# Local attention's output product: from sixteen full products to seven half-size block products per column group, with the work behind it moved into the scheduler

## The chip, the cores and the metric

The kernel runs on one core of one Trainium2 chip. The metric is the device time of one execution in microseconds (us), the median of three runs; lower is better. Five engines of the core work side by side, each through its own list of instructions in a fixed order: TensorE (PE in the rows) multiplies matrices, VectorE (DVE) and GpSimd (POOL) do elementwise work, ScalarE (ACT) does activations and copies, and SyncE (SP) issues most of the transfers (DMA). An instruction waits at the head of its engine's list until what it needs is there, and what stands behind it waits with it.

## The reference

The reference is one decoder block over 1024 positions of width 1024 in float32. Local attention (A, eight heads of 64 in a window of 128) and latent attention (B, eight heads) both read projections of the normed input; each has an output product, a gate, and the gated sum goes through one more product before a feed-forward part:

```
o_a = swa_sink_attention(qa, ka, va, swa_sinks[l])
o_b = mla_attention(q_nope, q_rope, k_nope, k_rope, vb)
y = jax.nn.sigmoid(g_a) * (o_a @ w_o_swa[l]) + jax.nn.sigmoid(g_b) * (o_b @ w_o_mla[l])
x = x + y @ w_out[l]
h = rmsnorm(x, ffn_norm_g[l])
x = x + (jax.nn.silu(h @ w_gate[l]) * (h @ w_up[l])) @ w_down[l]
```

`o_a` and `o_b` are 1024 x 512, `w_o_swa` and `w_o_mla` 512 x 1024, `w_out` 1024 x 1024.

## The kernel before

Every float32 operand of a product is split into a high and a low part in the engine's own number format: ACT casts the high part, DVE or POOL subtracts it from the source for the low part (`split`, and `lower` inside the scheduler). A product of two such operands is three matmuls per 128 rows of the contraction (`mm3`): high by high, high by low, low by high. A matmul has 128 x 128 weights and 512 columns. So "12 matmuls" below are one block of 128 x 512 outputs with a contraction of 512, and "6 matmuls" one with a contraction of 256.

The program goes through these stages, in us of the profiled execution:

- up to 318: projections, and the heads of local attention between products for the gates (`fa`, `fb`);
- 318 to 352: the plan `pre`: transposes of the latents (`lT`), rope products (`r`), the last gate products (`fb` with weights `wl`). The gate products are copied out of PSUM by ACT (`go`) and stored to `gate_d`;
- 352 to 531: latent attention, 8 heads by 8 query blocks, issued by `plan`. A block is a score product (`scb`), the row maximum (DVE), exp (ACT, `p`), a scale (POOL), transposes (`pTb`) whose results are split (`pth` by ACT, `ptl` by DVE), and the product with the values (`ob`). Between them stand the last products of queries and keys, and the output product of local attention, called oA: eight of its sixteen outputs (`mix_steps`, `G`), each 12 matmuls, copied out by ACT to `ar`;
- 531 to 599.8: the loop `steps`, written out by hand: the other eight oA (`mix_a`) and the sixteen outputs oB of latent attention (`mix_b`). There `gate` rows are loaded (`sg`), put through a sigmoid by ACT, multiplied by oA (four whole rows by POOL, L1847, eight halves by DVE, L1500) and by oB (DVE, L1852), added (DVE, L1853), split into `yh` and `yl`, and summed into the block sums of y (DVE, `y_sums`). `W_WORK` builds the block sums of `w_out` (tiles `wo`) beside it: loads, negations by ACT, and accumulating transfers (`w_acc`, from POOL's queue: the destination is added to in flight);
- from 599.8: the product with `w_out`, called xo, as seven block products over sums of blocks of y and w_out, and then the feed-forward part.

`Plan` is a list scheduler in the program that writes the kernel: every step has an engine, a cost in ns, the steps it follows, a rank and pool slots that it takes and gives back; the order in which the steps are picked is the order of the instructions on each engine. A load of weights is a step of SP with a cost of 400 ns (`w0`). The time at which the chip really does a step plays no part in it. `U` and `V` are two pools of SBUF slots.

## Time and profile before

| what | value |
|---|---|
| median of 3 runs | 1321.35 us (1320.81 to 1322.18) |
| the profiled execution | 1320.95 us, of which the span from the first to the last instruction is 1319.2 us and 1.75 us lie around it |
| PE, busy | 1306.1 us, 99% of the span |
| DVE, ACT, POOL, busy | 70%, 49%, 43% |
| mean granted clock of TensorE | 0.997 of full speed |

The profile comes from one execution. A busy share says how much of the span an engine worked; with PE at 99% the time is above all the number of matmuls times the pitch from one to the next, and what can be had beside that are PE's few gaps.

### The profile page before, as it was taken

The page shows a single profiled execution, that of the slowest core. Times are in us where ns is not written, and L with a number is a line of the kernel's source. Part 1 is how long each engine was busy: PE and PEld are TensorE (multiplying, and loading weights), DVE is VectorE, ACT ScalarE, POOL GpSimd, SP SyncE. Part 2 cuts the span into 40 slices and gives each one's busy share as a digit, 9 for nine tenths or more (in the row PEclk, how much of TensorE's full clock was granted, in tenths as well). Part 3 has the DMA queues.
Part 4 walks back from the last instruction along what each step waited for, and adds up shares of the span by engine and source line. Part 5 has one row for each costly group of instructions (what it writes and reads, how often), then busy time and mean ns, then how long its engine had stood idle before and what let it go on. Part 6 is the DMA issues. An engine that isn't in the chain of part 4 may idle for free.

```text
span 1319.2 us, 18715 instructions
## 1 busy us (share of the span) xinstructions
PE 1306.1 (99%) x6463; PEld 1102.4 (84%) x6463; DVE 919.9 (70%) x1514; ACT 643.2 (49%) x1301; POOL 566.4 (43%) x552
## 2 busy tenths in 40 slices
PE   9999999999999999999999999999999999999997
PEld 6899888887888888888888888888888888888886
DVE  7869777765778885589889755766566555663962
ACT  7434666665477787545464322232223323644452
POOL 2116666553333267310134467775566621022520
PEclk9999999999999999999999999999999999999999
DMA  9454332436410022896231336743454335996503
GB/s 375 161 187 154 117 111 85 132 105 211 143 30 17 25 81 81 309 265 191 84 124 49 126 139 222 260 178 133 180 183 162 134 119 201 386 361 225 178 24 134
DMA packets 81246, 210.49 MB, mean 160 GB/s; under 512 B 9408, under 2 KB 16064, under 8 KB 80448
## 3 DMA queue, kind: packets, MB, share of 16 engines
q1 hardware_dynamic: 78416, 202.48, 43.4%
q0 software_dynamic: 1440, 4.72, 1.9%
q10 hardware_dynamic: 1296, 2.10, 0.5%
q8 instruction: 51, 0.84, 0.3%
q14 instruction: 43, 0.35, 0.1%
HBM read 143.34 MB, written 61.73 MB: 155 GB/s over the span
## 4 chain that ended last, share of the span: by engine, by line
PE 96%; DVE 1%; issue 1%; ACT 1%; DMA 1%; POOLq 0%; POOL 0%; SPq 0%; ACTq 0%; DVEq 0%
PE fa L269 8%; PE fa L267 8%; PE fa L268 8%; PE fb L267 6%; PE fb L269 6%; PE fb L268 6%; PE fd L268 5%; PE fd L267 5%; PE fd L269 5%; PE pTb L1580 2%; PE xo L268 2%; PE xo L267 2%; PE xo L269 2%; PE ob L1618 1%; PE scb L1535 1%; PE ob L1617 1%
## 5 line engine op out<-in xcount | busy, mean ns | idle before, releaser
L261 DVE TENSOR_TENSOR wl<-wr,wl 128x512 fp32r<-128x512 f32 x147 | 143.4, 997 | 67.6 <-ACT wl L260 67.2
L261 DVE TENSOR_TENSOR lrv<-lr,lrv 128x1024 fp32r<-128x1024 f32 x77 | 105.1, 1396 | 49.6 <-ACT lrv L260 48.2
L260 ACT CAST lrv<-lr 128x1024 fp32r<-128x1024 f32 x77 | 80.2, 1052 | 95.2 <-PE fd L269 70.7
L267 PE MATMUL fd<-lrv 128*128 128x512 f32 x308 | 119.8, 389 | 0.0
L268 PE MATMUL fd<-lrv 128*128 128x512 f32 x308 | 119.8, 389 | 0.0
L269 PE MATMUL fd<-lrv 128*128 128x512 f32 x308 | 119.8, 389 | 0.0
L260 ACT CAST wl<-wr 128x512 fp32r<-128x512 f32 x147 | 85.2, 620 | 3.6 <-DVE wr L962 1.7
L1564 POOL TENSOR_SCALAR p<-p,denb 128x384 f32<-128x384 f32 (+3 forms) x64 | 47.9, 750 | 86.8 <-DVE denb L1560 72.2
L261 DVE TENSOR_TENSOR wl<-sm,wl 128x512 fp32r<-128x512 f32 x59 | 52.1, 907 | 35.1 <-ACT wl L260 35.0
L275 POOL TENSOR_TENSOR wr<-wr,sm 128x512 f32<-128x512 f32 x20 | 30.5, 1529 | 97.5 <-DVE wl L261 97.5
L267 PEld LDWEIGHTS fd<-lrv 128*128 128x128 f32 x308 | 57.8, 188 | 12.1
L269 PEld LDWEIGHTS fd<-lrv 128*128 128x128 f32 x308 | 57.8, 188 | 12.0
L268 PEld LDWEIGHTS fd<-lrv 128*128 128x128 f32 x308 | 57.8, 188 | 11.9
L397 POOL TENSOR_SCALAR ms<-ss 128x1 f32<-128x1 f32 x32 | 10.4, 324 | 112.8 <-ACT xn L2131 62.8
L2043 ACT ACTIVATE act<-sm 128x512 f32<-128x512 f32 x11 | 7.0, 633 | 104.1 <-DVE sm L272 104.1
L272 DVE TENSOR_TENSOR ptl<-pTb,pth 128x512 fp32r<-128x512 f32 (+2 forms) x96 | 49.5, 548 | 8.7 <-ACT pth L1591 8.4
L275 POOL TENSOR_TENSOR sm<-wr,wr 128x512 f32<-128x512 f32 (+1 forms) x36 | 41.6, 1162 | 30.6 <-PE fb L269 26.1
L1555 ACT ACTIVATE p<-scb,nmb 128x384 f32<-128x384 f32 (+3 forms) x64 | 47.8, 748 | 13.0 <-DVE nmb L1550 9.0
L1550 DVE CUSTOM_DVE_ANT_0 scb<-scb,mask 128x384 f32<-128x384 f32 (+3 forms) x64 | 48.3, 760 | 6.9 <-PE scb L1537 6.3
L267 PE MATMUL fb<-t3h,wl 128*128 128x512 f32 x120 | 48.1, 401 | 0.0
L1591 ACT CAST pth<-pTb 128x512 fp32r<-128x512 f32 (+2 forms) x96 | 43.1, 484 | 9.9 <-PE pTb L1580 9.4
L268 PE MATMUL fb<-t3l,wl 128*128 128x512 f32 x120 | 47.4, 395 | 0.0
(403 smaller groups left out, 4258.1 us busy)
## 6 DMA issues: line engine op xcount, KB each, us to landing
lr<-la_d SPq DMA_DIRECT2D x77, 256.0 KB, 5.4
wr<-in_w_gate_dram SPq DMA_DIRECT2D x22, 512.0 KB, 4.4
wr<-in_w_up_dram SPq DMA_DIRECT2D x22, 512.0 KB, 5.1
la_d<-sd SPq DMA_DIRECT2D x22, 512.0 KB, 5.1
wd<-in_w_down_dram SPq DMA_DIRECT2D x22, 512.0 KB, 6.5
rb_d<-wd SPq DMA_DIRECT2D x22, 512.0 KB, 2.6
lr<-rb_d SPq DMA_DIRECT2D x44, 256.0 KB, 5.4
lr<-in_w_down_dram SPq DMA_DIRECT2D x33, 256.0 KB, 5.4
```

The lines of the kernel that those rows point to most:

```text
L260: nc.scalar.copy(hi, src)
L261: (eng or nc.vector).tensor_tensor(lo, src, hi.bitcast(F32), op=ALU.subtract)
L267: nc.tensor.matmul(ps, ah, bh, start=first and i == 0, stop=False, skip_group_check=go_on)
L268: nc.tensor.matmul(ps, ah, bl, start=False, stop=False, skip_group_check=go_on)
L269: nc.tensor.matmul(ps, al, bh, start=False, stop=last and i == n - 1, skip_group_check=go_on)
L272: eng.tensor_tensor(out, a, b, op=ALU.subtract)
L275: eng.tensor_tensor(out, a, b, op=ALU.add)
L1550: nc.vector.tensor_tensor_reduce(s_, s_, m_, 1.0, -NEG, op0=ALU.add, op1=ALU.min, accum_out=nm)
L1555: nc.scalar.activation(p_, s_, AF.Exp, scale=-1.0, bias=t_.pop(("nm", key)), accum_out=den)
L1564: nc.gpsimd.tensor_scalar(p[:, 0:w], p[:, 0:w], den, 0.0, op0=ALU.mult, op1=ALU.add)
L1580: nc.tensor.transpose(pp[:, k], t_["p", key][:, blk(4 * g + k)], ident)
L1591: nc.scalar.copy(hi, pp)
```

## The change

The product oA is computed as seven block products per group of 128 output columns, in place of four full-size blocks of sums: the contraction of 512 and the 1024 positions are both cut in two, and sums of blocks of `o_a` (seven operand sets) are multiplied by sums of blocks of `w_o_swa`. There are four pairs of column blocks (j), so 28 products of 6 matmuls. The operand sets are made during the first heads of latent attention (`set_steps`): `oa` is loaded, POOL makes eight block differences (`os`), ACT and POOL split the seven sets (`oh`, `ol`), SP stores them to DRAM (`set_d`, 14 stores) and fetches them before use (`oas`, seven loads of 1 MB). Per j, POOL makes the sums of the weights (`wsum`, four operations), and these are split too. The seven products are added up on their way out of PSUM (`block_out`): two copies by ACT and five adds by DVE.

Everything of the hand-written loop becomes steps of `plan` (`post_steps`): loads of gates and sigmoids, all eight multiplications of a gate row by oA on POOL, the oB products, the sums, the splits of y, the block sums of y (half as additions on POOL, half as accumulating transfers from POOL's queue) and the sums of `w_out` with their splits, whose low parts go to POOL. The engine "Q" in the plan stands for the accumulating transfers. The plan now counts slots of U and V; slack and ranks are other numbers; the first xo product takes its low parts of y last.

```diff
-    TAIL = {"E": 0, "D": 80, "A": 100, "P": 36, "S": 0}
-    HOP = {"E": 70, "D": 36, "A": 36, "P": 79, "S": 50}
+    TAIL = {"E": 0, "D": 80, "A": 100, "P": 36, "S": 0, "Q": 8500}
+    HOP = {"E": 70, "D": 36, "A": 36, "P": 79, "S": 50, "Q": 0}
...
+                        if sum(x < busy for x in slots[pool]) < n + self.more[name][2]:
+                            t = busy
...
-    for nm, dp in (("oa", 0), ("oa", 1), ("oa", 2), ("ob", 0), ("ob", 1), ("oa", 3), ("ob", 2), ("ob", 3)):
+    for nm, dp in (("oa", 0), ("oa", 1), ("oa", 2), ("oa", 3), ("ob", 0), ("ob", 1), ("ob", 2), ("ob", 3)):
...
-    pre = Plan(30)
+    pre = Plan(0)
...
-    plan = Plan(30)
+    plan = Plan(45)
-    LOW = {'Q': 'P', 'u': 'P', 'o': 'P', 'b': 'P', 'w': 'P'}
+    LOW = {'Q': 'P', 'u': 'P', 'o': 'P', 'b': 'P', 'w': 'P', 'n': 'D', 'os': 'P', 'ws': 'P', 'Ba': 'D', 'ya': 'P', 'y': 'D', 's': 'P'}
...
+    R_HALF = {1: (0, 0), 2: (2, 0), 4: (2, 1)}
+    S_OF = {5: 0, 6: 1, 7: 2, 3: 3}
+    SET_OF = {1: (0, 0), 2: (1, 0), 3: (1, 1)}
+    A_ORDER = (1, 6, 2, 7, 5, 4, 3)
+    A_BANK = {1: 1, 2: 1, 6: 6, 7: 6, 4: 6, 5: 5, 3: 5}
+    oa_set = {}
+
+    def weight_sums(r, s, k, eng):
+        a11, a21, a12, a22 = r[:, 0:2, 0:P], r[:, 0:2, P:], r[:, 2:4, 0:P], r[:, 2:4, P:]
+        if k == 0:
+            add(s[:, 0], a21, a22, eng)
+            sub(s[:, 2], a11, a21, eng)
+        else:
+            sub(s[:, 1], s[:, 0], a11, eng)
+            sub(s[:, 3], a12, s[:, 1], eng)
+
+    def block_product(ps, q, w, start):
+        hi, lo = w[q not in R_HALF]
+        if q in R_HALF:
+            c0, f = R_HALF[q]
+            lhs = [(hi[:, c0 + c, blk(f)], lo[:, c0 + c, blk(f)]) for c in range(2)]
+        else:
+            lhs = [(hi[:, S_OF[q], c], lo[:, S_OF[q], c]) for c in range(2)]
+        hi, lo = oa_set[q]
+        mm3(ps, [(lhs[c], (hi[:, c], lo[:, c])) for c in range(2)], first=start, go_on=not start)
...
+    def set_steps(x, dx, xl, dxl):
+        raw_, parts = {}, {}
+
+        def load(g, sh):
+            raw_[g, sh] = U("oar", F32, (P, 2, 512))
+            nc.sync.dma_start(raw_[g, sh], oa_d[2 * g + sh])
...
+        def sums(n, dst, a, b, after, x):
+            for c in range(2):
+                add_step("os", n, c, x=x + 0.1 * c, eng=LOW["os"], port=True, cost=1290 if LOW["os"] == "P" else 700, free=(("oar", 0, 0),) if (n, c) == (4, 1) else (),
...
+            def store():
+                for i, t in enumerate(parts.pop(q)):
+                    nc.sync.dma_start(set_d[q][:, i], t.bitcast(F32))
+
+            def fetch():
+                t = V("oas", F32R, (P, 2, 2, 512))
+                nc.sync.dma_start(t.bitcast(F32), set_d[q])
+                oa_set[q] = t[:, 0], t[:, 1]
...
+        load_step(0, 0, x, [('vl', 7)])
+        load_step(0, 1, x, [("o0", 0, 0)])
+        load_step(1, 1, x + dx, [("o0", 0, 1)])
+        load_step(1, 0, x + 3 * dx, [("o0", 1, 1)])
+        one(1, (0, 0), [("o0", 0, 0)], x, 0)
+        sums(1, (0, 0), (0, 1), (0, 0), [("ol", 1), ("o0", 0, 1)], x + dx)
+        one(5, (0, 0), [("os", 1)], x + dx, 4)
+        sums(2, (0, 0), (1, 1), (0, 0), [("ol", 5), ("o0", 1, 1)], x + 2 * dx)
+        one(6, (0, 0), [("os", 2)], x + 2 * dx, 1)
+        sums(3, (0, 1), (1, 1), (0, 1), [("os", 1), ("o0", 1, 1)], x + 3 * dx)
+        one(7, (0, 1), [("os", 3)], x + 3 * dx, 3)
+        one(3, (1, 1), [("os", 2), ("os", 3)], x + 4 * dx, 6)
+        one(2, (1, 0), [("o0", 1, 0)], x + 5 * dx, 2)
+        sums(4, (1, 0), (1, 0), (0, 0), [("ol", 2), ("os", 2)], x + 6 * dx)
+        one(4, (1, 0), [("os", 4)], x + 6 * dx, 5)
...
+        def am(dc):
+            nc.gpsimd.tensor_tensor(gate[dc], ar.pop(dc), gate[dc], op=ALU.mult)
...
+        def y_sum(k, n, eng):
+            if not y_new:
+                y_new.append(V("ys"))
+            a21, a11, a22, a12 = y[k][:, half(1)], y[k][:, half(0)], y[4 + k][:, half(1)], y[4 + k][:, half(0)]
+            s1 = y_new[0][:, k]
+            if n % 2 == 0:
+                add(*((s1, a21, a22), None, (a11, s1, a11))[n], eng)
+            else:
+                dst, src = ((a21, a11), (a12, a11))[n // 2]
+                nc.gpsimd.dma_start(dst, src, accum_op=ALU.add)
...
+            nc.gpsimd.dma_start(wr[name][:, k], src_, accum_op=ALU.add)
...
-        add_step("w0", *key, x=x - 4, eng="S", cost=400, emit=load, after=[("S", *divmod(x - 4, NB)), *PROJ_LAST])
-        lower("w", key, x, (1050, 1224, 2400), lambda: part(0), lambda: part(1), lambda: t_["pw", key],
-              [("w0", *key), ("S", *divmod(min(x, NT - 1), NB))])
...
+        add_step("w0", *key, x=x - 4, eng="S", cost=400, emit=load, use=(("U", ("pw", *key)),), spare=5,
+                 after=[("S", *divmod(min(int(x) - 4, NT - 1), NB)), *PROJ_LAST])
+        kind = "w" if name == "oa" else "n"
+        lower(kind, key, x, (1050, 1224, 2400), lambda: part(0), lambda: part(1), lambda: t_["pw", key],
+              [("w0", *key), ("S", *divmod(min(int(x), NT - 1), NB))], use=[("U", ("w", *key, k)) for k in range(2)], spare=2)
...
+            lower("w", ("s", i), x + 1.5, (1050, 1224, 2400), lambda: part2(0), lambda: part2(1), lambda: t_["ws", i], [("ws", i, 1)],
...
-    for k in range(8):
-        swa_steps(k)
-        mix_steps(k)
-    proj_steps("oa", 0, NT - 17)
-    proj_steps("oa", 1, NT - 9)
-    proj_steps("oa", 2, NT + 0)
-    proj_steps("ob", 0, NT + 1)
+    set_steps(2.57, 3.85, NT + -14.73, 1.33)
+    block_steps(0, NT + -12.34, 1.087349035459975)
+    block_steps(1, NT + 3.75, 1.087349035459975)
+    block_steps(2, NT + 12.41, 1.087349035459975)
+    block_steps(3, NT + 2.98, 1.087349035459975)
+    proj_steps("oa", 0, NT + -16.95)
+    proj_steps("oa", 1, NT + -6.17)
+    proj_steps("oa", 2, NT + -5.71)
+    proj_steps("oa", 3, NT + -1.44)
+    proj_steps("ob", 0, NT + -1.19)
+    proj_steps("ob", 1, NT + 4.78)
+    proj_steps("ob", 2, NT + 11.05)
+    proj_steps("ob", 3, NT + 14.19)
+    post_steps(5.84, 2.03, (10.84, 12.72, 19.65, 17.64))
...
-        if dc < 4:
-            wo["b"] = st.get(("ob", dc))
-        w = wo["b"]
-        ga, gb = gate.pop(dc), gate.pop(8 + dc)
-        if dc < 4:
-            nc.gpsimd.tensor_tensor(ga, ar.pop(dc), ga, op=ALU.mult)
...
-        s1 = y_new[0][:, k]
-        add(s1, a21, a22, nc.vector)
-        add(a21, a11, a21, nc.vector)
-        add(a11, s1, a11, nc.vector)
-        add(a12, a11, a12, nc.vector)
...
-    steps = ("a4", "b0", "b4", "a5", "b1", "b5", "a6", "b2", "b6", "a7", "b3", "b7")
...
+        ps = bank["A" if q in (1, 2, 5, 3) else "B"][t]
+        if (q, t) == (1, 0):
+            for k in range(4):
+                nc.tensor.matmul(ps, ah[:, k, blk(t)], bh[:, k], start=k == 0, stop=False)
+                nc.tensor.matmul(ps, ah[:, k, blk(t)], bl[:, k], start=False, stop=False)
+            for k in range(4):
+                nc.tensor.matmul(ps, al[:, k, blk(t)], bh[:, k], start=False, stop=k == 3)
```

In all PE has 6436 matmuls in place of 6460, DVE 1508 instructions (1516), ACT 1146 (1136), POOL 610 (552) and SP 576 (555), as counted in the two programs.

Three places show how the instructions move. The first is on TensorE, in the plan `pre` near 321 us. `lT` are transposes of the latents, `fb` the twelve matmuls of a gate product with weights `wl_3718`; a number behind a name tells buffers apart. Before:

```order
L1243 MATMUL lT_3787<-ident,lat_3678 128x128
L1243 MATMUL lT_3796<-ident,lat_3672 128x128
L1243 MATMUL lT_3796<-ident,lat_3674 128x128
L1243 MATMUL lT_3796<-ident,lat_3676 128x128
L1243 MATMUL lT_3796<-ident,lat_3678 128x128
L1243 MATMUL lT_3804<-ident,lat_3672 128x128
L1243 MATMUL lT_3804<-ident,lat_3674 128x128
L1243 MATMUL lT_3804<-ident,lat_3676 128x128
L1243 MATMUL lT_3804<-ident,lat_3678 128x128
L267 MATMUL fb_3720<-t3h_1080,wl_3718 128x512
L268 MATMUL fb_3720<-t3l_1081,wl_3718 128x512
L269 MATMUL fb_3720<-t3h_1080,wl_3718 128x512
```

and after the change, at the same place:

```order
L1245 MATMUL lT_3787<-ident,lat_3676 128x128
L1245 MATMUL lT_3787<-ident,lat_3678 128x128
L269 MATMUL fb_3720<-t3h_1080,wl_3718 128x512
L270 MATMUL fb_3720<-t3l_1081,wl_3718 128x512
L271 MATMUL fb_3720<-t3h_1080,wl_3718 128x512
L269 MATMUL fb_3720<-t3h_1080,wl_3718 128x512
L270 MATMUL fb_3720<-t3l_1081,wl_3718 128x512
L271 MATMUL fb_3720<-t3h_1080,wl_3718 128x512
```

The twelve `fb` matmuls, of which the first six are shown, now stand ahead of the two sets of transposes that they followed.

The second is on ScalarE at the end of latent attention. `wh` is the high part of weights (`wr`: loaded, `wsum`: sums), `pth` the cast of transposed probabilities, `sg` a gate row. Before:

```order
L1808 COPY ar_6205<-oA_6259 128x512
L1591 CAST pth_6297<-pTb_6275 128x4x128
L1591 CAST pth_6300<-pTb_6281 128x128
L1808 COPY ar_6284<-oA_6283 128x512
L1591 CAST pth_6297<-pTb_6305 128x4x128
L1591 CAST pth_6300<-pTb_6311 128x2x128
L1808 COPY ar_6284<-oA_6318 128x512
L1808 COPY ar_6342<-oA_6341 128x512
```

and after:

```order
L1624 CAST wh_6300<-wr_6289 128x1024
L1571 CAST pth_6333<-pTb_6304 128x128
L1571 CAST pth_6333<-pTb_6306 128x2x128
L1534 ACTIVATE p_6309,denb_6338<-scb_6293,nmb_6310 128x768
L1478 ACT_TABLE_LOAD
L1478 ACTIVATE sg_6312<-sg_6312 128x1024
L1603 COPY otb_6358<-ob_6279 64x512
L1757 COPY ar_6362<-oA_6351 128x512
L1478 ACTIVATE sg_6349<-sg_6349 128x1024
L1478 ACTIVATE sg_6373<-sg_6373 128x1024
L1759 COPY ar_6361<-oA_6351 128x512
L1571 CAST pth_6401<-pTb_6388 128x4x128
```

The cast of a just loaded weight tile (`wr_6289`, the third of `w_o_swa`), the table load and the sigmoids now stand among the last casts of attention; before they stood ahead of all of it or behind all of it.

The third is on GpSimd in the stage of the oB products. `sg<-ar,sg` multiplies a gate row by oA, `wol` is the low part of a block sum of `w_out`, `ys` and `sg<-sg` on lines 277 and 1871 are the block sums of y, "DMA" is the issue of an accumulating transfer. Before, the whole stage:

```order
L272 TENSOR_TENSOR obT_6384<-ob_5989,obT_6384 128x512 x2
L1847 TENSOR_TENSOR sg_6393<-ar_5828,sg_6393 128x1024
L1847 TENSOR_TENSOR sg_6470<-ar_6205,sg_6470 128x1024
L1847 TENSOR_TENSOR sg_6598<-ar_6284,sg_6598 128x1024
L1895 DMA wo_6516<-wo_6468 128x1024 x2
L1895 DMA wo_6468<-in_w_out_dram 128x1024 x2
L1847 TENSOR_TENSOR sg_6727<-ar_6342,sg_6727 128x1024
L1895 DMA wo_6596<-wo_6468 128x1024 x2
L1895 DMA wo_6725<-wo_6596 128x1024 x2
```

and after, a piece from its middle:

```order
L277 TENSOR_TENSOR ys_6726<-sg_6312,sg_6373 128x512
L1871 DMA sg_6312<-sg_6312 128x512
L1922 DMA wo_6614<-wo_6570 128x1024 x2
L1841 TENSOR_TENSOR sg_6741<-ar_6501,sg_6741 128x1024
L274 TENSOR_TENSOR wol_6795<-wo_6647,woh_6794 128x1024
L277 TENSOR_TENSOR sg_6312<-ys_6726,sg_6312 128x512
L1922 DMA wo_6647<-wo_6614 128x1024
L274 TENSOR_TENSOR wol_6795<-wo_6647,woh_6794 128x1024
L1871 DMA sg_6373<-sg_6312 128x512
L277 TENSOR_TENSOR ys_6726<-sg_6632,sg_6696 128x512
L1922 DMA wo_6647<-wo_6614 128x1024
L1841 TENSOR_TENSOR sg_6832<-ar_6502,sg_6832 128x1024
```

POOL's list grows from fourteen instructions in this stage to some forty, and gate multiplications stand in it behind transfers and sums.

## Rows read from the trace of the kernel before

**Rows 1.** The page's first view: the span, and busy time, share and count of TensorE.

```profile
span 1319.2 us, 18715 instructions
PE 1306.1 (99%) x6463; PEld 1102.4 (84%) x6463; DVE 919.9 (70%) x1514; ACT 643.2 (49%) x1301; POOL 566.4 (43%) x552
```

**Rows 2.** The chain of work that ended last, by engine, share of the span.

```profile
PE 96%; DVE 1%; issue 1%; ACT 1%; DMA 1%; POOLq 0%; POOL 0%; SPq 0%; ACTq 0%; DVEq 0%
```

**Rows 3.** One third of the matmuls of oA, oB, xo: durations, first and last start.

```profile
L267 PE MATMUL oA<-wv,wh x64: 387/389/484, 486.9 to 588.3; 128*128 128x512 f32 x64
...
L267 PE MATMUL oB<-obT,wh x64: 389/389/389, 540.0 to 599.1; 128*128 128x512 f32 x64
...
L267 PE MATMUL xo<-woh,yh x112: 389/389/476, 599.8 to 678.9; 128*128 128x512 f32 x112
```

**Rows 4.** Timeline of PE (start, us, instruction): first and last of 25 512-column matmuls.

```profile
311.71 0.39 PE L267 MATMUL fa<-hh,wl 128*128 128x512 f32 x1
...
317.15 0.39 PE L269 MATMUL fb<-t2h,wl 128*128 128x512 f32 x1
```

**Rows 5.** Timeline of PE, 321 to 329; brackets: idle before it, and who ended it.

```profile
321.46 0.60 PE L1243 MATMUL lT<-ident,lat 128*128 128x128 f32 x4
324.06 1.18 PE L1243 MATMUL lT<-ident,lat 128*128 128x128 f32 x8 [2.00 <-ACT go L972]
324.91 0.76 PE L267 MATMUL fb<-t3h,wl 128*128 128x512 f32 x1
...
328.42 0.40 PE L269 MATMUL fb<-t3h,wl 128*128 128x512 f32 x1
```

**Rows 6.** Timelines of DVE (the low part of those `fb` weights) and ACT (the copy).

```profile
316.41 0.69 DVE L272 TENSOR_TENSOR wl<-wr,wl 128x512 fp32r<-128x512 f32 x1
...
323.41 0.60 ACT L972 COPY go<-fa 128x512 f32<-128x512 f32 x1
```

**Rows 7.** Windows: length, busy of PE, PEld, DVE, ACT, POOL; clock, DMA share, GB/s.

```profile
324.00:328.00 4.00, 3.94 (x15) 3.32 (x16) 2.66 (x5) 1.61 (x4) 0.00 (x0) 0.62 0.60 197
...
352.00:415.00 63.00, 62.30 (x378) 54.40 (x377) 50.87 (x122) 47.17 (x104) 17.80 (x23) 1.00 0.18 52
480.00:520.00 40.00, 39.47 (x260) 35.88 (x261) 28.75 (x76) 34.74 (x78) 34.57 (x32) 1.00 0.13 41
531.00:600.00 69.00, 69.00 (x309) 57.27 (x309) 51.26 (x66) 35.83 (x43) 18.42 (x13) 1.00 0.91 289
```

**Rows 8.** Transfers, 440 to 520 (first row) and 520 to 640: median us to landing.

```profile
wr<-in_w_o_swa_dram SPq DMA_DIRECT2D x3, 512.0 KB, 3.3
...
wo<-wo POOLq DMA_DIRECT2D x6, 512.0 KB, 9.7
wr<-in_w_o_mla_dram SPq DMA_DIRECT2D x3, 512.0 KB, 5.8
```

**Rows 9.** Groups by shape, 340 to 640: count, busy us, mean ns, idle before.

```profile
L1484 ACT ACTIVATE sg<-sg 128x1024 f32<-128x1024 f32 x16 | 15.9, 1048 | 4.5 <-DMA sg<-gate_d 4.5
...
L261 DVE TENSOR_TENSOR wol<-wo,woh 128x1024 fp32r<-128x1024 f32 x10 | 12.1, 1219 | 1.3 <-ACT woh L260 1.3
...
L272 POOL TENSOR_TENSOR wv<-oar,wv 128x512 fp32r<-128x512 f32 x8 | 10.2, 1288 | 0.6 <-ACT wv L1641 0.5
...
L1847 POOL TENSOR_TENSOR sg<-ar,sg 128x1024 f32<-128x1024 f32 x4 | 9.6, 2400 | 14.5 <-DMA sg<-gate_d 10.4 <-ACT sg L1484 4.1
```

**Rows 10.** Timeline of POOL in the stage of oB.

```profile
555.28 2.40 POOL L1847 TENSOR_TENSOR sg<-ar,sg 128x1024 f32<-128x1024 f32 x1 [10.38 <-DMA sg<-gate_d]
557.62 1.98 POOL L1895 DMA_DIRECT2D wo<-wo  x2
566.01 0.86 POOL L1895 DMA_DIRECT2D wo<-in_w_out_dram  x1 [6.41 <-DMA wo<-wo]
```

**Rows 11.** Timeline of DVE at the same place: two sums of y, both operands in SBUF.

```profile
553.42 0.69 DVE L275 TENSOR_TENSOR ys<-sg,sg 128x512 f32<-128x512 f32 x1
...
555.36 2.87 DVE L275 TENSOR_TENSOR sg<-ys,sg 128x512 f32<-128x512 f32 x1
```

More of the change, by code (lines that the diff above doesn't have):

```diff
@@ L1690, in prod @@
                                           (ckv[k][0][:, half(s)], ckv[k][1][:, half(s)])) for k in range(2)])
-        add_step("K", j, s, x=x, eng="E", emit=prod, cost=1360, take=("p", ("k", j, s), 1), after=[("S", 2 * j - 2, NB - 1)] + [("K", j, 0)] * s)
+        add_step("K", j, s, x=x, eng="E", emit=prod, cost=1360, take=("p", ("k", j, s), 1), after=[("S", 2 * j - 2, NB - 1)] + [("K", j, 0)] * s, free=[("ckv", k) for k in range(2)] * (s and j == 3) + [("wk",)] * (s and j == 3))
         for u in range(2):
@@ L1711, in load @@
             wuq[j] = {}
-        add_step("u0", j, x=x - 8, eng="S", cost=400, emit=load, after=[("vl", 3)])
+        add_step("u0", j, x=x - 8, eng="S", cost=400, emit=load, after=[("vl", 3)], use=(("U", ("uq", j)),))
         for u in range(2):
```

333 lines of the change are left out of this document (188 added, 145 removed).

## The prediction

> **What bounds the kernel now.** I read the page's first view and the chain of waits first: TensorE is busy 1306.1 of 1319.2 us [rows 1], and 96% of the chain that ends last is its work [rows 2]. So time is worth looking for in two things only: how many matmuls there are, and where TensorE waits or runs at the lower clock. The tiles give the stages: oA from 486.9 to 588.7, oB from 540.0, xo from 599.8 [rows 3]. The pitch of a 512-column matmul comes from the timeline: 25 of them start between 311.71 and 317.15, so 24 pitches take 5.44 us, 0.2267 us each [rows 4]; 6 matmuls take 1.36 us and 12 take 2.72.
>
> The windows then show where TensorE is not full. From 531 to 600 it has no gap, 69.00 of 69; in 352 to 415 and 480 to 520 it lacks 0.7 and 0.5 us [rows 7]. The one place that stands out is near 322: four transposes start at 321.46, the next eight only at 324.06, 2.00 us of it idle, released by ACT's copy `go`, and the matmuls behind come slowly [rows 5]. ACT's copy runs from 323.41 to 324.01 [rows 6], so it is this copy that is late and not a semaphore. In that window the granted clock is 0.62 on the mean [rows 7]: part of it at 1.2 GHz, the lower level, after TensorE had stood idle.
>
> **The matmuls removed.** Before, oA is 64 matmuls on each of three lines [rows 3], 192. After, 4 column pairs x 7 products x 6 make 168. 24 x 0.2267 = **-5.44 us**. The stage has no idle time into which this could vanish, and nothing else on TensorE is added.
>
> **The order in `pre`.** After the change the twelve `fb` matmuls start behind `lT_3787`, ahead of the transposes that waited. They need 2.72 us; the wait was 2.00. The low part of their weights is done at 317.1 [rows 6], so they can start near 321.8, end near 324.5, and the copy is done at 324.01. The wait goes: 2.00 us. The slow clock goes with it if it came of the wait: from 324.91 to 328.42 eight pitches took 3.51 us [rows 5], against 8 x 0.2267 = 1.81, a loss of 1.70. Together **-3.70 us**. ACT's list before the copy is the same, so the copy itself is not earlier; bounds are 0 (the `fb` waits for something that the old order hid) and -3.70.
>
> **The operand sets.** POOL gets 8 differences and 14 low parts of 1.29 us (the low parts of `oa` took 1288 ns [rows 9]), 28 us, less the eight low parts that it made before. They are spread over the first heads, where POOL is busy 17.8 of 63 us [rows 7]. In 480 to 520 the same mix of splits and scales held POOL at 34.6 of 40 us, and TensorE still worked 39.47 [rows 7]; so I take 0. Without that cover a scale would come up to 1.29 us late, and a transpose behind it. The 14 stores and 7 fetches find the DMA engines at a share of 0.18 and 0.13 [rows 7]: 0 as well.
>
> **The tail of attention.** Before, full-size oA products with operands long ready filled the last blocks. After, weights come just in time. The third load of `w_o_swa` is issued when the fourth product of the first column pair frees a slot. It lands 3.3 us later when the DMA engines are quiet, 5.8 us when they are not [rows 8]; the plan counts 0.4. On ACT its cast (1.05 us, as a 128x1024 activation [rows 9]) stands ahead of the last short casts `pth`, and those ahead of the last product with the values. TensorE has between release and need 24 matmuls of 256 columns, 6 of 384 and 7 of 128: 9344 columns, at the pitch 4.1 us. Needed are 3.3 + 1.05 and about half a us of short casts: 4.9, or 7.4 with the slow landing. So 0.8 to 3.3 us of wait; I take 1.3, since that stretch is still quiet. Behind it the table load and four sigmoids of 1048 ns [rows 9] stand between ACT's copies and casts: each of some four instructions that TensorE or a free PSUM bank depends on may come one sigmoid late, 0 to 4 us; I take 1.7, less than half, since TensorE has nine products of 1.36 us in between. Together **+3.0**, bounds 0 to 7.
>
> **From the first oB to xo.** Call the first oB start zero. TensorE has 16 x 2.72 + 7 x 1.36 = 53.0 us until xo. On POOL the sums of `w_out` form a chain of four issues, each of which waits for the landing before it: 9.7 us [rows 8], and 0.86 to 0.99 us for the issue itself [rows 10]. That this queue stops POOL's list is in the trace already: 6.41 us of idle time ahead of an issue, released by such a transfer [rows 10]. There it cost nothing, for DVE made the sums of y; after, gate multiplications and sums stand behind it. 4 x 10.6 = 42.4 us from some 3 us after zero: 45.5. Behind it two gate multiplications of 2.40 [rows 9]: 50.3. Then two sums on DVE, a cast and a low part, each about 0.69 [rows 11]: 53.0. Due is the last low part of the first set at 53.0 + 11 x 0.2267 = 55.5, since xo's first product takes low parts last.
>
> What these DVE steps can lose is in the trace: a sum took 0.69 us at 553.42 and 2.87 at 555.36 [rows 11], where POOL's 2.40 us multiplication ran from 555.28 to 557.68 [rows 10]. It ended with POOL's plus its own time, so an operation of DVE with both operands in SBUF waits for one of POOL. The Trainium skill says so too (GPSIMD Engine Reference, Specifications: the SBUF interfaces are shared, with contention for DVE instructions with two SBUF inputs); it speaks against moving work to POOL, gives no price, and the trace agrees. With three such steps in the chain it is 0 to 3 x 2.40 late: from 2.5 us early to 4.7 late; I take 1.0. The second set hangs on the eighth gate multiplication, behind two sums and another landing, at about 61.6; with 2.7 us behind it 64.3, and up to 7.2 later; due at 53.0 + 10.9 + 2.0 = 65.9. I take 1.5. Together **+2.5**, bounds 0 to 10.
>
> A page would have it otherwise. The Trainium skill (DMA: Bandwidth & Descriptors, Anatomy of one DMA) gives 2.0 us plus the bytes at 436 GB/s for a transfer of POOL's queue, an estimate of 3.2 us for 512 KB. The rows show 9.7, three times that, under a DMA share of 0.91; by the page the term would be 0.
>
> **The sum**, against the profiled execution: 1319.2 + 1.75 = 1320.95; -5.44 - 3.70 + 3.0 + 2.5 = -3.64; 1317.3. The median is 0.4 above that execution: **1317.7 us**.
>
> **The rivals.** (a) *Everything is covered*: the loads land at 3.3 us and the casts are in time, DVE's waits fit into slack. For it: no gap at all in 531 to 600 with DVE at 51 of 69 us [rows 7]. Against: POOL had 18 us of work there, and gets over 60. -9.14: 1312.2.
> (b) *POOL's list becomes the bound*, on the other side. Sums of y on POOL wait at the head of its list for accumulating transfers of y, as the issues do for those of `w_out`. If only two more landings come one after the other and not side by side, gate multiplications slip by 2 x 9.7 = 19 us, of which some 4 are slack: xo starts 15 late, the net is -9.14 + 3.0 + 15, +9: 1330. It decides for slower when the stage loses more than 8.8 us (-9.14 + 3.0 + 8.8 = +2.64). For it: the 6.41 us of waiting [rows 10] with a quarter of the instructions. Against: the transfers of y and of `w_out` are independent of each other.
> (c) *The order in `pre` gains nothing*: the wait shows up before `fb` or before the rope products behind. For it: ACT is as late as before. Against: the copy ends 0.5 us before the twelve matmuls do. 1317.7 + 3.7 = 1321.4, no change.
> (d) *Accumulating transfers land early*, as quiet loads do, in 3.3 us [rows 8]: the chain of four is 4 x 4.2 = 17 us and POOL's own work decides, 5 multiplications and 5 low parts of 2.40, 3 sums of 1.29 and 11 issues, 38 us, well ahead of 50. The term of 2.5 goes: 1315.2. This is what the page named above would give.
>
> **How the numbers follow.** The forecast has 0.45, with a range of its own of 1314 to 1321; (a) 0.22, (b) 0.15, (c) 0.13, (d) 0.05. A measurement of this kernel can tell about 0.2%, 2.64 us, from no change. Faster by more, below 1318.7: 0.27 of the forecast's 0.45, all of (a) and (d), 0.02 of (c): 0.56. Slower, above 1324.0: (b) and 0.01 of the rest, 0.16. Between: 0.28. The range from 1311.5 to 1323.5 leaves (b) out above and little of (a) below.
>
> **What would show it.** 168 oA matmuls, at the old pitch, show the first term. Near 322 the `fb` matmuls follow four transposes without idle time, and the granted clock of 324 to 328 is 1.00. In the last 15 us before the first oB the waits name `ptl`, `pth` or `ar`, about 3 us in all; at the start of xo and of its second product they name `yl`. The first oB to xo then takes 53 to 56 us. Wrong would be: TensorE idle over 3 us at one place with the clock down behind it, a wait of oB for PSUM, or a POOL list that runs on into xo by more than 10 us.

## The result and the profile after

| kernel | median of 20 runs | lowest to highest | ratio to before, 95% interval |
|---|---|---|---|
| before | 1320.61 us | 1318.80 to 1323.19 | |
| after | 1326.59 us | 1319.89 to 1328.81 | 1.0035 [1.0027, 1.0043] |

The changed kernel is 0.35% slower, 4.6 us by the ratio. The forecast was 1317.7 with a range up to 1323.5, so the sign is wrong. The scatter has grown too: 8.9 us between the shortest and the longest run, against 4.4. The profiled execution took 1319.98 us, nearly the shortest of the twenty, so it doesn't show what the median pays. A second profile of the same kernel (the first experiment) fell on 1326.28 us and is the typical one. Both are read below, and told apart as the short one and the typical one. The page's first view, of the short one, then the span of the typical one:

```profile
span 1318.3 us, 18794 instructions
...
PE 1302.5 (99%) x6439; PEld 1096.3 (83%) x6439; DVE 934.9 (71%) x1506; ACT 650.6 (49%) x1311; POOL 642.3 (49%) x610
```

```profile
span 1324.6 us, 18794 instructions
```

TensorE has 24 matmuls fewer than in [rows 1] and is busy 3.6 us less; POOL is busy 76 us more. The tiles of the typical profile, which answer to [rows 3]:

```profile
L269 PE MATMUL oA<-oas,wh x56: 387/391/504, 494.3 to 573.1; 128*128 128x512 f32 x56
...
L269 PE MATMUL oB<-obT,wh x64: 389/389/632, 545.2 to 603.1; 128*128 128x512 f32 x64
...
L2275 PE MATMUL xo<-woh,yh x4: 389/389/389, 603.8 to 605.2; 128*128 128x512 f32 x4
```

oA is 3 x 56 = 168 matmuls, as the change says. One oB matmul took 632 ns where before the longest took 389. xo starts at 603.8, before at 599.8. Who made TensorE wait (the five longest waits of the typical profile from 310 to 720: total, times, longest):

```profile
PE oB L269 <- DVE sg L1850: 3.6, 1, 3.6
PE scb L1514 <- DMA qT<-rq_d: 1.7, 1, 1.7
PE xo L2278 <- DVE yl L274: 1.1, 1, 1.1
PE oA L269 <- DVE ptl L274: 0.9, 1, 0.9
PE oA L269 <- ACT ar L1757: 0.7, 1, 0.7
```

Together they are 8.0 us, and none of the five was there before. The largest is an oB product that waits for a bank of PSUM (the memory into which TensorE writes its results): line 1850 is DVE's multiplication of a finished oB by a gate row, which gives the bank back. DVE and POOL around it in the typical profile, with start, duration and instruction:

```profile
584.54 8.71 DVE L274 TENSOR_TENSOR yl<-sg,yh 128x512 fp32r<-128x512 f32 x1
593.17 0.68 DVE L1850 TENSOR_TENSOR sg<-oB,sg 128x512 f32<-128x512 f32 x1
```

```profile
584.61 2.70 POOL L274 TENSOR_TENSOR wol<-wo,woh 128x1024 fp32r<-128x1024 f32 x1
586.96 1.19 POOL L1871 DMA_DIRECT2D sg<-sg  x1
587.57 1.91 POOL L277 TENSOR_TENSOR ys<-sg,sg 128x512 f32<-128x512 f32 x1
588.82 1.50 POOL L1922 DMA_DIRECT2D wo<-wo  x1
589.42 3.27 POOL L1841 TENSOR_TENSOR sg<-ar,sg 128x1024 f32<-128x1024 f32 x1
592.69 0.87 POOL L1871 DMA_DIRECT2D sg<-sg  x1
```

```profile
593.90 0.50 PE L269 MATMUL oB<-obT,wh 128*128 128x512 f32 x1 [3.63 <-DVE sg L1850]
...
607.59 0.50 PE L2278 MATMUL xo<-woh,yl 128*128 128x512 f32 x1 [1.10 <-DVE yl L274]
```

This is the core of the case. One subtraction on DVE, of the same shape as the sum that took 0.69 us in [rows 11], took 8.71: it ran from 584.54 to 593.25, through a row of POOL's work without a gap, and ended 0.56 behind the last arithmetic in it (589.42 + 3.27 = 592.69). The multiplication `sg<-oB,sg` stood behind it on DVE, TensorE waited 3.63 us for that, and the granted clock fell. The windows of the typical profile (length; busy PE, PEld, DVE, ACT, POOL; clock; DMA share; GB/s):

```profile
352.00:415.00 63.00, 60.84 (x372) 53.16 (x371) 49.74 (x122) 50.10 (x112) 39.45 (x42) 1.00 0.48 161
...
520.00:545.20 25.20, 23.31 (x108) 17.98 (x108) 10.09 (x16) 15.32 (x21) 21.71 (x16) 1.00 0.49 186
...
545.20:588.00 42.80, 42.80 (x190) 35.44 (x189) 29.50 (x32) 21.15 (x24) 28.04 (x19) 1.00 1.03 317
588.00:603.80 15.80, 12.17 (x47) 9.57 (x46) 15.80 (x14) 6.65 (x9) 11.31 (x9) 0.89 1.05 301
```

From the first oB to 588 TensorE had no gap, at a clock of 1.00. From 588 to 603.8 it worked 12.17 of 15.80 us at a mean clock of 0.89 of full speed, which is a part of it at 1.2 GHz. Before, the whole stage had no gap [rows 7].

The short profile has the same kind of operation at another place:

```profile
551.72 8.39 DVE L277 TENSOR_TENSOR sg<-sg,sg 128x512 f32<-128x512 f32 x1
560.04 0.68 DVE L277 TENSOR_TENSOR ar<-oA,ar 128x512 f32<-128x512 f32 x1
```

```profile
560.77 0.50 PE L269 MATMUL oA<-oas,wh 128*128 128x512 f32 x1 [1.66 <-DVE ar L277]
```

There it cost 1.66 us of waiting. The lists of all engines are the same in the two profiles, so the stall moves from execution to execution, and what it costs hangs on what is queued behind it. That goes with the wide scatter.

The accounts by stage: for every matmul of the trace I take the pitch to the next less what its columns need at the upper clock (columns / 2.4 GHz + 13 ns: 0.227 us for 512, which is the pitch of [rows 4]; I give the 13 ns, left there over 512 / 2.4 GHz, to every matmul); the rest is TensorE's lost time: waiting, slow clock, and what matmuls of fewer columns take beyond this formula. A stage runs from its first matmul to the next stage's first.

| lost time of TensorE, us | up to `lT` | `pre` | attention and first oA | oB to xo | xo to feed-forward |
|---|---|---|---|---|---|
| before | 14.65 | 6.14 | 22.15 | 0.01 | 3.37 |
| after, short profile | 15.39 | 2.61 | 27.61 | 2.00 | 3.33 |
| after, typical profile | 15.83 | 2.77 | 28.25 | 5.57 | 4.79 |

The typical profile against before: -5.44 for the matmuls, -3.37, +6.10, +5.56, +1.42, and +1.18 in the first stage, where the program is unchanged: +5.45; the spans differ by 5.4.

### The profile page after: what moved, and what is told of

It is laid out like the page before. It is cut to its first block, busy times and chain, and to the rows that moved or that the text cites. A ratio compares the mean times of both kernels' runs of the same rounds, so it can differ in the third digit from the quotient of the medians.

```text
span 1318.3 us, 18794 instructions
## 1 busy us (share of the span) xinstructions
PE 1302.5 (99%) x6439; PEld 1096.3 (83%) x6439; DVE 934.9 (71%) x1506; ACT 650.6 (49%) x1311; POOL 642.3 (49%) x610
## 4 chain that ended last, share of the span: by engine, by line
PE 67%; DVE 2%; issue 2%; POOL 2%; ACT 1%; DMA 1%; SPq 0%; POOLq 0%; ACTq 0%; DVEq 0%
PE fa L271 6%; PE fa L269 6%; PE fa L270 6%; PE fd L270 5%; PE fd L269 5%; PE fd L271 5%; PE fb L271 4%; PE fb L269 4%; PE fb L270 4%; PE xo L270 2%; PE xo L269 2%; PE xo L271 2%; PE pTb L1560 2%; PE ob L1599 1%; PE scb L1514 1%
## 5 line engine op out<-in xcount | busy, mean ns | idle before, releaser
L263 DVE TENSOR_TENSOR wl<-wr,wl 128x512 fp32r<-128x512 f32 x147 | 147.9, 1028 | 67.8 <-ACT wl L262 67.4
L277 POOL TENSOR_TENSOR du<-du,xq 128x512 f32<-128x512 f32 x8 | 16.3, 2054 | 69.5 <-DVE du L277 69.5
L2165 ACT ACTIVATE act<-pu 128x512 f32<-128x512 f32 x22 | 13.9, 632 | 68.9 <-DVE pu L274 38.5
```

Of the source, the lines that this page charges most:

```text
L263: (eng or nc.vector).tensor_tensor(lo, src, hi.bitcast(F32), op=ALU.subtract)
L277: eng.tensor_tensor(out, a, b, op=ALU.add)
```

## The experiments

Ratios are to the kernel before, run on the same chip beside it, with 95% intervals. The expectations of the first three runs weigh late loads and ACT's order (L), the rows of the queries (Q) and POOL's list ahead of xo (P). From the typical profile on, three theories of the stall stand against each other. **S** (lock-out): an operation of DVE with both operands in SBUF, the on-chip memory for operands, can't run while POOL works through SBUF without a pause, and what hangs behind it on DVE costs the time; **S2** is its narrower form, that DVE gets in only where POOL's row has a gap. **W**: it waits for one POOL operation, as the prediction had it. **L** (loads): the oB stage is late because the loads and accumulating transfers are late, and DVE only shows it.

**The same kernel again, the order in `pre` alone, and all but that order.** The second is the kernel before with the changed numbers of `pre`, the third the changed kernel with the old ones (likewise `XS`):

```diff
-    pre = Plan(30)
-    PRANK = {'Ql': 3.986179849961461, 'bh': -1.7271477738298369, ...
+    pre = Plan(0)
+    PRANK = {'Ql': 0.22915986068655436, 'bh': -8.05315971136043, ...
```

> The changed kernel once more, to see what its usual execution looks like: its runs went from 1319.9 to 1328.8 us, and the profiled one was among the shortest. Theory L (late loads and the order on ScalarE at the end of attention): the profile shows some 5 us more idle time and slow clock between 505 and 562 than the first one did. Theory Q (the rope rows of the queries near 356): the wait of 1.75 us there is longer and the clock falls behind it. Theory P (POOL's list holds up xo): waits of xo for its y operands after 598.

1325.83 us, ratio 1.0037 [1.0024, 1.0050]; its profile is the typical one above. None of the three theories named the wait of oB. Q's wait is no longer than in the short profile (1.7 us), and P's, of xo, is there with 1.1.

> The kernel before with the new numbers of the plan `pre` alone (slack, ranks, times). The idle 2.00 us at 324 and the slow clock behind it go, 3.7 us. Theories L and P: nothing is lost elsewhere, 3.5 us faster than before. Theory Q: the wait for the rope rows near 356 comes with these numbers, 1.8 us or more, so 0 to 2 us faster, or slower by 1 to 3 where the clock falls behind that wait.

1319.9 us, ratio 0.9994 [0.9985, 1.0003]: in the middle 0.8 us faster, and not to be told from nothing.

> The changed kernel with the old numbers of the plan `pre`. Theories L and P: 3.7 us slower than the changed kernel, the wait at 324 is back and all else stays. Theory Q: the wait at 356 is gone with them, so as fast as the changed kernel or up to 3 us faster.

1327.82 us, ratio 1.0049 [1.0037, 1.0061]. The wait at 322 is back (2.39 us, released by the same copy `go`), and the stall stands where it stood: 8.73 us on `yl<-sg,yh` at 584.08, and 3.72 us of waiting at oB.

So the order in `pre` doesn't cause the loss. It does what was predicted at its place. The first two rows are the kernel after, short profile; the last is the third experiment's, with the old order:

```profile
322.20 0.60 PE L1245 MATMUL lT<-ident,lat 128*128 128x128 f32 x4
322.55 0.48 PE L269 MATMUL fb<-t3h,wl 128*128 128x512 f32 x1
```

```profile
324.51 1.09 PE L1245 MATMUL lT<-ident,lat 128*128 128x128 f32 x8 [2.39 <-ACT go L974]
```

The `fb` matmuls follow at once, with no wait as in [rows 5]. But `pre` now ends some 2 us earlier, and something else is not ready. PE and SP of the short profile near 358:

```profile
358.36 0.47 PE L1514 MATMUL scb<-kT,qT 96*128 96x512 f32 x1 [1.75 <-DMA qT<-rq_d]
```

```profile
350.73 2.12 SPq L1346 DMA_DIRECT2D kT<-kT  x2
352.94 8.96 SPq L1352 DMA_DIRECT2D qT<-rq_d  x12
```

The rotated rows of the queries come back from DRAM through loads that SP issues at some 0.75 us each, behind two copies of key rows that took 2.12 us to issue. A score product waits 1.75 us for them. With the old order (third experiment) that wait is gone; with the new order alone (second) it is 0.92. The old order takes 2.1 us in `pre` (4.89 lost, 2.77 with the new) and gives 1.5 back in attention (26.71 and 28.25).

**What POOL does to DVE, by itself.** Two kernels that hold nothing but rows of such operations: DVE adds 128x512 tiles while POOL adds 128x1024 tiles. The lines that matter, from the second; "T" is an addition on POOL, "D" (the `else`) the issue of an accumulating transfer, "g" a tiny operation:

```diff
+            if what in "Tt":
+                g = gs[0 if what == "t" else k]
+                nc.gpsimd.tensor_tensor(g, x0, x1, op=ALU.add)
...
+            elif what == "g":
+                d = tiny("gap")
+                nc.gpsimd.tensor_scalar(d, g[:, 0:1], 1.0, None, op0=ALU.mult)
+            else:
+                nc.gpsimd.dma_start(free.pop(), x1[:, 0:512], accum_op=ALU.add)
...
+            nc.vector.tensor_tensor(v, x0[:, 0:512] if what == "S" else ps, x1[:, 0:512], op=ALU.add)
```

> The disputed cost by itself: no part of the block is computed. In eight pieces DVE does additions of 128x512 with both operands in SBUF (with one in PSUM in the sixth piece) while POOL does none, one, two, four additions in a row, three with two issues of accumulating transfers between them, four, six, and four with three issues between. Theory S (an addition of DVE with both operands in SBUF waits until POOL's unbroken row of work ends): the second addition takes 0.69, about 1, 3, 8, 6 us; in the sixth piece 0.69 each; in the last two 12 and 9 us. Theory W (it waits for the one POOL operation that is running): never over 3.1 us, and the second, third and fourth each get one.

With DVE alone an addition took 0.68 us. Beside one POOL operation the first took 1.25; beside rows of two and four POOL additions, each of which waits for the one before, 2.82 each; with issues of transfers between, 3.40 and 3.28. The two longest rows had one DVE addition each, of 1.25, and say nothing more. With an operand in PSUM it took 0.68 to 0.69 throughout. So one DVE operation waits about one POOL operation, as I had priced it, and 8.7 us is not explained by this.

> The probe again, now with POOL additions that write to different buffers and so wait for nothing of their own (in the first probe each waited for the one before it, which left a gap of 0.08 us). No part of the block is computed. Pieces: four such additions, six, three with two issues of accumulating transfers between, four into one buffer, four beside DVE additions with an operand in PSUM, four multiplications by one scalar per row, four with a tiny operation that reads the result behind each. Theory S2 (DVE gets in only where POOL's row has a gap): DVE's second or third addition takes about 10 us in the first piece, 15 in the second, 8 in the third, 2.8 in the fourth and the seventh, 0.69 in the fifth. Theory W: 2.8 to 3.4 us everywhere but in the fifth.

Here the POOL operations don't wait for each other. Plain rows of four and six gave 1.25, 2.82, 2.82 again, not the 10 us and more that an unbroken row should give by S2. The row T D T D T gave something else. DVE, then POOL, of that row:

```profile
36.65 1.25 DVE L276 TENSOR_TENSOR secondc<-x,x 128x512 f32<-128x512 f32 x1
37.82 2.82 DVE L276 TENSOR_TENSOR thirdc<-x,x 128x512 f32<-128x512 f32 x1
40.57 6.66 DVE L276 TENSOR_TENSOR fourthc<-x,x 128x512 f32<-128x512 f32 x1
```

```profile
40.04 1.03 POOL L272 DMA_DIRECT2D acc<-x  x1
40.82 2.64 POOL L262 TENSOR_TENSOR pool<-x,x 128x1024 f32<-128x1024 f32 x1
43.10 1.19 POOL L272 DMA_DIRECT2D acc<-x  x1
43.71 2.95 POOL L262 TENSOR_TENSOR pool<-x,x 128x1024 f32<-128x1024 f32 x1
```

6.66 us: the addition began just ahead of an operation of POOL, and ended only behind the second one, 47.23 against 46.66. That is the picture of 584.54 in small, in one operation of one execution. In this probe rows of additions took turns with DVE; the one row of additions with issues of transfers between, of which none waits, didn't. Four additions into one buffer gave 1.25, 2.82 and 2.82 as before, four POOL multiplications by one scalar per row 1.25, 0.68 and 1.52, and additions with an operand in PSUM 0.68. With a tiny operation that depends on the one before (g) between the additions, nothing took longer than 2.82.

**Taking the work off POOL.** The low parts of the sums of `w_out` on DVE; the block sums of y on DVE, their accumulating transfers too; both:

```diff
-    LOW = {... 'ya': 'P', 'y': 'D', 's': 'P'}
+    LOW = {... 'ya': 'P', 'y': 'D', 's': 'D'}
```

```diff
-    LOW = {... 'ya': 'P', 'y': 'D', 's': 'P'}
+    LOW = {... 'ya': 'D', 'y': 'D', 's': 'P'}
...
-                nc.gpsimd.dma_start(dst, src, accum_op=ALU.add)
+                add(dst, src, dst, nc.vector)
```

> The changed kernel with the low parts of the w_out sums on DVE again (four operations of 2.40 us leave POOL, four of 1.22 go to DVE); TensorE's order is the same. Theory S: POOL's rows are shorter, about half of the wait of 3.6 us before an oB goes: 1322 to 1324.5. Theory L (the fourth load of w_o_mla lands 8.0 us after its issue, and the rest follows from it): no difference, 1325 to 1327. Theory W: 1 us faster.

1323.4 us, ratio 1.0019 [1.0007, 1.0031]; the runs still lie 9.0 us apart. The wait of oB is gone, and the longest DVE operation of the stage is down to 4.05 us. But that one stands right ahead of xo, and the wait is now there:

```profile
602.39 0.50 PE L2275 MATMUL xo<-woh,yh 128*128 128x512 f32 x1 [3.35 <-ACT yh L1624]
```

```profile
597.63 4.05 DVE L277 TENSOR_TENSOR sg<-sg,sg 128x512 f32<-128x512 f32 x1 [3.12 <-POOL sg L1841]
```

Ahead of that operation DVE stood idle 3.12 us for a gate multiplication of POOL. So part of this wait is POOL's list running late, and not the lock-out.

> The changed kernel with the block sums of y as sixteen additions on DVE again, no accumulating transfers of y and none of its eight additions on POOL; TensorE's order is the same. Theory S: 1321 to 1324, the rows of POOL work get gaps. Theory L: no difference, or 0.5 us less. Theory P (POOL's list is the bound): xo no longer waits for its low parts, 1.1 us and the clock behind it, 1323 to 1325.

1327.6 us, ratio 1.0045 [1.0032, 1.0058]: no gain. POOL's low parts, gate multiplications and issues of `w_out` still stand close together; an operation of 8.38 us stands at 554.80, where the short profile has its own, and xo waits 2.6 us for `yh`.

> Both moves together: POOL is left with the eight gate multiplications and the accumulating transfers of w_out. Theory S: the waits of 3.6 and 1.1 us and the slow clock behind them go, 1318 to 1320.5, and the runs scatter as little as those of the kernel before. Theory L: 1325 to 1327 still. Theory D (DVE becomes the bound with 16 us more work): a wait of oB for PSUM stays, 1323 to 1327.

1322.48 us, ratio 1.0010 [1.0001, 1.0018]. No wait of oB; one DVE operation of 4.88 us beside two gate multiplications of POOL, and 1.75 us of waiting for `yl` at xo. DVE's row, then POOL's:

```profile
586.19 4.88 DVE L277 TENSOR_TENSOR sg<-ys,sg 128x512 f32<-128x512 f32 x1
```

```profile
585.41 5.10 POOL L1841 TENSOR_TENSOR sg<-ar,sg 128x1024 f32<-128x1024 f32 x2
```

Here no issue stands between the two multiplications, and DVE was held through both (to 591.07, against 590.51). So the issues aren't needed for a hold over more than one operation, though plain rows in the probe never gave one. What differs between the two is not shown.

**Leaving all the work where it is and only putting gaps into POOL's row.** Behind each gate multiplication, each low part of `w_out` and each addition of y, POOL gets one more operation, on one column of what it has just made, so that it must wait for it. Nothing is taken away, and no load moves: beside the twenty tiny operations, the lists of all engines are those of the changed kernel, instruction by instruction.

```diff
+        def gap(t):
+            d = tiny("gap")
+            nc.gpsimd.tensor_scalar(d, t[:, 0:1], 1.0, None, op0=ALU.mult)
...
             nc.gpsimd.tensor_tensor(gate[dc], ar.pop(dc), gate[dc], op=ALU.mult)
+            gap(gate[dc])
```

> The changed kernel with a tiny POOL operation behind each gate multiplication, each low part of a w_out sum and each addition of y on POOL; it reads one column of the result, so that POOL waits for its own work before it goes on. Nothing is moved to another engine; POOL gets 20 more instructions of 0.1 to 0.3 us. Theory S2: the additions of 8.4 to 8.7 us on DVE are gone, 2.8 to 3.4 at most, and the wait of 3.6 us before an oB with them: 1321 to 1324. Theory L or P: no faster, POOL has more to do: 1326 to 1329.

1320.87 us (1320.01 to 1322.47), ratio 0.9998 [0.9989, 1.0007]. Against the changed kernel's ratio of 1.0037 that is 0.39%, 5.1 us, for work that was only added. POOL and DVE of that kernel:

```profile
560.54 2.68 POOL L274 TENSOR_TENSOR wol<-wo,woh 128x1024 fp32r<-128x1024 f32 x1
563.32 0.55 POOL L1844 TENSOR_SCALAR gap<-wol 128x1 f32<-128x1 f32 x1
563.82 0.92 POOL L1932 DMA_DIRECT2D wo<-in_w_out_dram  x1
564.46 2.71 POOL L1849 TENSOR_TENSOR sg<-ar,sg 128x1024 f32<-128x1024 f32 x1
```

```profile
561.85 1.94 DVE L277 TENSOR_TENSOR sg<-sg,sg 128x512 f32<-128x512 f32 x1
564.31 3.43 DVE L274 TENSOR_TENSOR yl<-sg,yh 128x512 fp32r<-128x512 f32 x1
```

The last row is the longest DVE operation of the stage. oB loses 0.01 us, as in the kernel before, and the eleven runs lie within 2.5 us. L falls with this: the transfers were not touched, and the loads of the gate rows even landed later (9.5 us at the median from 520 to 640, against 8.0 in the typical profile). What stands of S is this: the long holds came where nothing on POOL waited, and a dependent operation behind each large one ends them. That DVE gets in only at a gap, as S2 has it, the plain rows of the probe contradict. New waits come with the gaps: an oA product waits 1.1 us for a low part of POOL (`wl`), and xo 0.9 us for `yh`, some us after DVE stood idle 2.58 us for a gate multiplication. The kernel with gaps is level with the one before, and not ahead of it by the matmuls removed, since attention and the stage of xo still lose 7.0 and 2.0 us more than there.

> The kernel with both moves to DVE, and the tiny operation behind each gate multiplication. Theory S2: the one addition of 4.9 us that was left goes: 1320.5 to 1322. Theory D (DVE's own work is the bound there): no difference, 1322 to 1323.

1323.84 us, ratio 1.0022 [1.0012, 1.0031]. The operation of 4.88 us is gone (the longest takes 3.03), but the wait for `yl` at xo stays, at 1.84 us. DVE now works without a pause from 585.3 to 606.5, most operations at 0.68 us: its own list is full there, and the gaps don't help (the ratio is 0.12% above that of both moves alone).

**What is left, from the kernel with gaps.** First, SP issues the copies of the key rows behind the loads that the score product waits for:

```diff
         for t in k_tiles:
-            if kT:
-                nc.sync.dma_start(t[64:QK].bitcast(F32), k_tiles[0][64:QK].bitcast(F32))
             kT.append((t[:, 0], t[:, 1]))
...
                 load_rope(h, s)
+            if (j, s) == (0, 1):
+                for t in k_tiles[1:]:
+                    nc.sync.dma_start(t[64:QK].bitcast(F32), k_tiles[0][64:QK].bitcast(F32))
```

> The kernel with the small POOL operations between, and in addition SyncE issues the two copies of the keys' rope rows to the other key tiles behind the loads of the queries' rope rows of heads 0 and 1, and not ahead of them. Nothing else moves. Theory (the wait of about 1.5 us of a score product near 356 is SyncE's issue order, the two copies took 2.15 us of issuing ahead of the twelve loads): the wait of scb on qT goes or falls below 0.3 us, and the time falls by 1.5 to 2 us against the kernel with gaps alone, to about 1319.1, ratio to the kernel before about 0.9985. Rival (another step ends there last, such as the splits of the query product or the transfers themselves): a wait of 1 us or more stays at the same place under another name and the time stays at about 1320.9.

1318.94 us, ratio 0.9990 [0.9982, 0.9999]. The wait is gone from the list (1.54 us in the kernel with gaps alone). SP's row:

```profile
349.03 0.86 SPq L1642 DMA_DIRECT2D kT<-kT  x1
351.00 3.33 SPq L1350 DMA_DIRECT2D qT<-rq_d  x4
354.43 0.54 SPq L1642 DMA_DIRECT2D kT<-kT  x1
```

The first four loads are issued by 354.33; one copy slipped ahead all the same. The ratio falls by 0.08%, 1.1 us, less than the 1.5 to 2 that were expected; the two intervals overlap, so the size is uncertain, though the wait itself is shown to hang on the issue order. This is the fastest version here: by the ratios about 1.3 us shorter than the kernel before and some 6 shorter than the changed one.

Second, beside that, the sigmoids of all but the first pair of gate rows follow the last cast of attention on ACT:

```diff
-                add_step("gs", i, x=x - 1.5, eng="A", cost=1000, emit=lambda i=i: sigmoid(i), after=[("g0", i), ("E", NH - 1, NB - 1)])
+                add_step("gs", i, x=x - 1.5, eng="A", cost=1000, emit=lambda i=i: sigmoid(i), after=[("g0", i), ("E", NH - 1, NB - 1)] + [("H", NH - 1, NB - 1, 1)] * (n > 0))
```

> The same kernel, and in addition all sigmoids of gate rows but those of the first pair follow the last cast of transposed probabilities on ScalarE, so that they no longer stand between the last short casts and copies of attention. Theory of the tail term (the two waits of oA near 523 and 529, 0.7 on ar and 0.9 on ptl, come of the sigmoids standing ahead on ScalarE's list): both go, and the time falls by another 1 to 1.6 us, to about 1317.8, ratio about 0.9975, if the gate multiplications that then come later on POOL have that slack. Rival (the sigmoids are needed by then, since POOL's list of some 60 us of work starts with the gate multiplications): the waits at 523 and 529 go, but the start of xo is late by as much or more, with waits on yh or yl, and the time is the same or up to 3 us longer.

1321.42 us, ratio 1.0008 [0.9999, 1.0017]: 2.4 us worse than the one ahead of it. Its four longest waits, from the longest of its eleven executions:

```profile
PE xo L269 <- DVE x L277: 2.1, 2, 1.3
PE xo L2286 <- DVE sg L1860: 2.0, 1, 2.0
PE oA L269 <- DVE ptl L274: 0.8, 1, 0.8
PE oA L269 <- ACT ar L1760: 0.7, 1, 0.7
```

The two waits in the tail of attention did not move, against the theory and its rival alike; the start of xo is late by 2.0 us, as the rival had it. The wait for `ptl` isn't made by these sigmoids: those that were moved stand behind it now, and it is still 0.8. The wait for `ar` stood behind the first sigmoid and its table load, which this edit leaves in place, so it says nothing of that one. The plan also put some instructions of other engines in another order, so not all of the 2.4 us need come of the sigmoids.

## Why the prediction was wrong, point by point

- **The matmuls removed, -5.44: right.** 168 oA matmuls at the old pitch, and 5.44 us less of matmul time in the accounts.
- **The order in `pre`, -3.70: right at its place, wrong in the sum.** `pre` loses 3.37 us less. Rival (c) looked for the wait "before `fb` or before the rope products behind", and not at what the end of `pre` hands on: the rows of the queries, whose loads SP issues one by one. They take back 1.5 to 1.7 us. Alone, in the kernel before, the order is worth 0.8 us (0 within its interval).
- **The operand sets, 0: nearly right.** Apart from the wait for `qT`, the windows show nothing above 0.4 us more of idle time in attention up to 520. By the account of lost time, of the 6.10 us more in the table some 1.3 lie around the wait for `qT` and 3.4 from 520 on; the other 1.4 belong to no wait above 0.6 us, and stay unexplained.
- **The tail of attention, +3.0: right in size, its causes not shown.** From 520 to the first oB, TensorE is idle 1.89 us and loses 3.4 us more than before by the account; the waits name `ptl` (0.9) and `ar` (0.7), as the prediction had it. Before, it had no gap from 520 to 540:

```profile
520.00:540.00 20.00, 20.00 (x103) 16.89 (x102) 3.28 (x6) 10.73 (x17) 3.82 (x3) 1.00 0.75 281
```

  The late cast of weights, priced at 1.3, shows as one wait of 0.3 us for `pth` at 519. Of the sigmoids, priced at 1.7, the last experiment moved seven pairs and neither wait changed.
- **From the first oB to xo, +2.5 with bounds 0 to 10: the step that failed.** Its words were that "an operation of DVE with both operands in SBUF waits for one of POOL", priced three times at 2.40 us at the end of the chain, where most of it met slack. Two things were missed. The wait isn't for one: where POOL runs operations and issues in a row without a wait, one DVE operation stood through all of it: 8.38 to 8.73 us in four profiles, and 4.88 through two multiplications in the kernel with both moves. And I followed only the chain that makes y; the DVE list also holds the multiplications that give oB's banks back, and TensorE waits for these in the middle of the stage, which I had taken as full. Measured: 5.56 us in the stage and 1.42 behind it, 7.0 where I had 2.5. The bounds would have held it; but 4.5 more here and the 1.7 of `qT` make 1323.9 of the 1317.7, which is out of the range, and the 1.2 us more of the first stage, where the program is unchanged, come on top.
- **The rivals.** (b) came out on the right side for another reason: what cost most is not that POOL's list runs late (with the gaps, which only lengthen it, oB loses nothing) but that it locks out DVE. Lateness shows at xo alone: 0.9 us with the gaps, and part of the 3.35 where the low parts went to DVE; the 15 us of (b) are nowhere. (c) is about half true. (a) is out, and so is (d): accumulating transfers landed after 8.8 us (`w_out`) and 7.9 us (y), and by DVE's rows neither of TensorE's waits for oB and xo leads back to them.

The text listed "TensorE idle over 3 us at one place with the clock down behind it, a wait of oB for PSUM" as what would make it wrong; it was just that. The trace of before could have warned of it: in [rows 11] a sum of 0.69 us took 2.87 beside a single operation of POOL, and the change put some forty instructions there, where [rows 10] shows POOL mostly waiting. How long such a row can hold DVE up, though, is in no row of before.

Shown by experiment: that breaking POOL's row gives the 5 us back with nothing taken away; that moving the low parts of `w_out` off POOL gives back part of it and moves the wait to xo, and that moving the sums of y alone gives back nothing; that the wait near 358 hangs on SP's order. Open: what lets DVE in between two operations of a plain row in the probe and not between two gate multiplications in the kernel, what part the issues of transfers have in it, what chooses the place of the stall in an execution, and what makes the waits for `ptl` and `ar`. No edit that broke the row with something other than a dependent operation was tried.

## What to carry to other kernels

Before elementwise work goes from DVE to POOL, look at what POOL's list is like there: a list that runs on without a wait held up one of DVE's SBUF operations for 8.7 us here, and that cost more than the 24 matmuls which the change had saved. Price it for whatever stands behind the blocked operation on DVE, above all the operations that free PSUM banks, and not only for the chain of data. And where a wait is taken out of one stage, look for the next thing that is made at the old time: here rows that SP fetches with twelve small loads.

## What the runs showed of the hardware that was not expected

- A DVE addition of 128x512 with both operands in SBUF took 0.68 us alone, 1.25 to 2.82 beside plain rows of POOL additions and, once, 6.66 where POOL alternates additions with issues of accumulating transfers. In the kernel such operations took up to 8.73 us, and 4.88 beside two multiplications with no issue between. With an operand in PSUM an addition took 0.68 to 0.69 beside rows of four POOL additions. The Trainium skill (GPSIMD Engine Reference, Specifications) says that the two engines share SBUF interfaces; the traces here agree, and these are their sizes.
- A POOL operation on one column, 0.21 to 1.07 us long, that depends on the one before it was enough to let DVE in; twenty of them took 5.1 us off the kernel.
- Issues cost the issuing engine's time: 8.96 us for twelve small loads on SP; on POOL 0.87 us for an accumulating transfer, and up to 1.50 while DVE was held up.
